# A fused decoder trunk's MLP weights rounded twice, once into SBUF and once into a PSUM bank for the subtraction

## The chip, the cores and the metric

The kernel runs on one core of one Trainium2 chip. The metric is the device time of one execution, in microseconds (us). Three runs of the kernel before gave 1218.43, 1218.79 and 1220.8 us; their median, 1218.79 us, is the time before.

## The reference

Two layers of a decoder trunk, all in fp32, on 512 tokens with a model width of 1024. Layer 0 mixes tokens by attention, layer 1 by a short gated convolution. Each mixer is followed by an MLP, and each sub-layer stands between two RMSNorms. The part that matters here is the MLP, 1024 to 4096 to 1024:

```python
def sq_relu_mlp(h, w_up, w_down):
    return jnp.square(jax.nn.relu(h @ w_up)) @ w_down
```

A norm scales each row by the inverse root of its mean square and by a gain vector; the MLP's input h is such a normed residual. A gated per-layer embedding closes each layer.

## The kernel before, in words

**Products.** TensorE multiplies in a rounded 32-bit type (fp32r) and the result has to be close to fp32, so every operand is held as a pair: `hi`, the value rounded to fp32r, and `lo`, what the rounding left out. `mm3` (L266 to L272) issues three matmuls for each product: hi·hi (L268), lo·hi (L269) and hi·lo (L270). It also counts the columns that TensorE has been given, and runs work that was put off until a given count.

**Splitting.** `split` (L274) makes a pair: ScalarE casts the source to `hi` (L276), and another engine, VectorE unless told otherwise, subtracts `hi` from the source to get `lo` (L277). Each 128 x 512 fp32 weight tile is split in this way; the trace calls its parts `raw`, `wh` and `wl`. The same two lines split the normed activations (`hTh`, `hTl`) and the MLP's hidden activations (`A11h`, `A12h`, `S1h`, `S3h` and their low parts).

**Weights.** All weight tiles stand in one list in the order of use. `wide` and `narrow` ask for a tile, and `prepare` (L175) then begins every tile up to eight (`SOON`) behind it: it fetches the raw tile by SP's DMA queue, takes two SBUF pages for hi and lo, and splits it. Raw tiles share 14 buffers.

**PSUM.** There are eight banks, each of 128 x 512 fp32. `bank` (L83) takes one for every product, transpose or attention step, and the framework gives it back after its last reader.

**The MLP** (`mlp`, L957). The 4096 hidden columns are worked through in eight groups of 512. In each, `up` computes four column blocks f, each of 8 k-tiles times three matmuls on 512 tokens into one bank, then ScalarE's Relu `r` (L975) and Square `q` (L961). Group 0 does this in two halves of 256 tokens, so that the first half can start before the last two token blocks are normed. Groups 0 to 6 multiply by the down weights with a Strassen-Winograd scheme of seven products. It takes sums of the hidden activations (`s`, made on GpSimd, L989) and of the down tiles (`T1` to `T4`, in the trace `dn_T`, made on GpSimd, L168). `down` (L1003) runs the products in the order 1, 2, 4, 5, 6, 7, 3; each takes two banks, called `dn_10`, `dn_11`, `dn_20` and so on, and four products of three matmuls. In group 0, ScalarE copies the two banks into `acc` pages (L1018); in groups 1 to 6, VectorE adds them there (L1021). Group 7 is plain. Eight of a group's fourteen down operands are such T pages. In groups 1 to 6 GpSimd makes their low parts; in group 0 VectorE does.

**Around the MLP.** Before layer 0's MLP, attention's output blocks are normed and added to the residual, block after block of 128 tokens (`om` L366 and `xb` L373 on VectorE). Then `pre_norm` (L344) takes the squares on ScalarE (L312), the inverse root on GpSimd (L307), and the scaled rows `n_h` (L328) on VectorE. TensorE transposes them into a bank `n_p` (L337), and `keep` splits that bank into hTh and hTl. The transposes are put off by a number of TensorE columns, so that TensorE has other work meanwhile. The first T page waits for the last n_h.

**What sets the order.** The program is written once, in order; a scheduler in the framework then places every engine's instructions into one fixed queue per engine by its own estimates. Each engine runs its queue in order, so an instruction that waits holds up everything behind it.

Of the kernel before, what the change touches and what calls it, by code (L numbers as in the profile page):

```python
# [9 lines left out]
F32R = mybir.dt.float32r  # L10
AF = mybir.ActivationFunctionType
ALU = mybir.AluOpType
# [56 lines left out]
def trunk(ctx: ExitStack, tc, x, xT, pT, g, gT, wv, wqk, bf, wo, wci, wcq, cw, wco, wup, wdn, wpp, wpg, out):  # L69
    nc = tc.nc  # L70
# [12 lines left out]
    def bank(name):  # L83
        return psum.tile([P, S], F32, tag="ps", name=name)
# [90 lines left out]
    def prepare(upto, lows=None):  # L175
        while begun[0] < min(upto, len(order)):
            n = begun[0]
            begun[0] += 1
            key, at = order[n]
            for of in (key[:3], key[:2]):  # L180
                if of in recipes:
                    derive(of)
            hi, lo = page(f"wh{n}", F32R), page(f"wl{n}", F32R)
            if isinstance(at, tuple):
                raw, w = derived.pop(key), S
                eng = nc.gpsimd if (key[0] == "dn" and key[2] > 0) or key[-1] in ON_POOL else nc.vector
            else:
                fetch(at + 1)
                raw, eng, w = fetched[at], lows or nc.vector, loads[at].shape[-1]
                fetched[at] = None  # L190
            if key[0] in ("v", "qk"):
                split_gained(hi, lo, raw, w, key[2], eng, key[0] == "qk" or key[1] == 2)
            else:
                split(hi[:, :w], lo[:, :w], raw[:, :w], eng)
            ready[key] = Pair(hi[:, :w], lo[:, :w])
# [78 lines left out]
    def split(hi, lo, src, eng=nc.vector):  # L274

        nc.scalar.copy(hi, src)  # L276
        return eng.tensor_tensor(out=lo, in0=src, in1=hi.bitcast(F32), op=ALU.subtract)  # L277

    def split_gained(hi, lo, src, w, at, eng, paired):

        parts = [(slice(0, w), at)]
        if paired:
            parts = [(slice(256 * i, 256 * i + 256), 2 * at + i) for i in range(2)]
        for c, k in parts:
            nc.scalar.mul(hi[:, c], src[:, c], first_g[:, k : k + 1])
        for c, k in parts:
            eng.scalar_tensor_tensor(
                out=lo[:, c], in0=src[:, c], scalar=first_g[:, k : k + 1],
                in1=hi[:, c].bitcast(F32), op0=ALU.mult, op1=ALU.subtract,
            )  # L290
# [1029 lines left out]
```

## Time and profile before

| what | value |
|---|---|
| runs | 1218.43, 1218.79, 1220.8 us |
| span of the profiled execution | 1216.5 us |
| median of the runs less this span | 2.3 us |
| TensorE (PE) busy | 1205.5 us, 99% |
| weight loads (PEld) busy | 1027.5 us, 84% |
| VectorE (DVE) busy | 931.4 us, 77% |
| ScalarE (ACT) busy | 691.4 us, 57% |
| GpSimd (POOL) busy | 655.4 us, 54% |
| HBM traffic | 120 GB/s over the span |

The profile is one execution; its own time is the span, and what lies around it (start and end of the program) is the difference from the runs' times. A group's row reads: line, engine, operation, output<-inputs, partitions x elements and types, count | busy time, mean ns of one | idle time of the engine just before them, and what ended most of it. A row of a timeline reads: start in us, length in us, engine, line, operation, count, and in brackets the idle time before it and what released it. A row of the waits reads: engine, instruction, what it waited for: us in total, times, longest. A row of windows gives each engine's busy time in a stretch of the span. A row of one line's instructions gives count, then minimum, median and maximum duration in ns, and the first and last start. Matmuls overlap, so one takes less time from start to start than its own length.

### The profile page before, as it was taken

Reading aid. Unit: us, or ns where it says so; the run is one execution under the profiler, and the core shown is the slowest. Engines: PE = TensorE matmul, PEld = TensorE weight load, DVE = VectorE, ACT = ScalarE, POOL = GpSimd, SP = SyncE. Lnnn points to the kernel's source line nnn. Section 1 sums busy time; section 2 is a strip of 40 time slices with the busy share of each in tenths; the row PEclk is TensorE's granted clock in tenths of the full one; section 3 lists DMA queues with packets and bytes.
Section 4 is the critical chain, followed back from the end, with each engine's and each line's share of the span. In section 5 each row is a group of like instructions: output and inputs, shape, how many; then the busy total and the mean of one; then the engine's idle time right before and its main releaser. Section 6 shows DMA issues by size and latency. Waiting matters only on the chain.

```text
span 1216.5 us, 18743 instructions
## 1 busy us (share of the span) xinstructions
PE 1205.5 (99%) x6175; PEld 1027.5 (84%) x6175; DVE 931.4 (77%) x1474; ACT 691.4 (57%) x1465; POOL 655.4 (54%) x616
## 2 busy tenths in 40 slices
PE   9999999999999999999999999999999999999997
PEld 8888887898888888888889999989888888888886
DVE  7888889586669766879877888866876787669873
ACT  7687778458644564455665534545746445645551
POOL 2035666155787877774213455126676878678210
PEclk9999999999999999999999999999999999999999
DMA  9376544623234323438223123542422443135401
GB/s 333 122 210 172 167 152 125 222 93 94 77 113 138 102 66 110 139 97 276 83 88 108 35 80 103 176 154 71 139 87 65 127 138 106 61 112 185 162 13 58
DMA packets 87314, 150.84 MB, mean 124 GB/s; under 512 B 10352, under 2 KB 18080, under 8 KB 87216
## 3 DMA queue, kind: packets, MB, share of 16 engines
q1 hardware_dynamic: 86640, 149.11, 39.3%
q8 instruction: 49, 0.80, 0.3%
q10 hardware_dynamic: 576, 0.53, 0.1%
q14 instruction: 49, 0.40, 0.1%
HBM read 139.03 MB, written 6.37 MB: 120 GB/s over the span
## 4 chain that ended last, share of the span: by engine, by line
PE 91%; ACT 3%; issue 2%; DVE 2%; POOL 1%; DMA 0%; SPq 0%; POOLq 0%; DVEq 0%; ACTq 0%
PE up L269 9%; PE up L270 9%; PE up L268 9%; PE dn L268 8%; PE dn L270 8%; PE dn L269 8%; PE v L476 3%; PE pg L269 2%; PE pg L268 2%; PE pg L270 2%; PE qk L270 2%; PE qk L269 2%; PE qk L268 2%; PE pT L590 1%; PE co L269 1%
## 5 line engine op out<-in xcount | busy, mean ns | idle before, releaser
L277 DVE TENSOR_TENSOR wl<-raw,wh 128x512 fp32r<-128x512 f32 x346 | 344.7, 1041 | 14.1 <-ACT wh L276 13.4
L269 PE MATMUL up<-hTh,wl 128*128 128x512 f32 (+1 forms) x576 | 210.2, 365 | 0.0
L270 PE MATMUL up<-hTl,wh 128*128 128x512 f32 (+1 forms) x576 | 209.6, 365 | 0.0
L268 PE MATMUL up<-hTh,wh 128*128 128x512 f32 (+1 forms) x576 | 208.7, 366 | 0.0
L276 ACT CAST wh<-raw 128x512 fp32r<-128x512 f32 x346 | 189.4, 625 | 4.5 <-DVE xd L373 4.4
L975 ACT ACTIVATE r<-up 128x512 f32<-128x512 f32 (+1 forms) x72 | 39.5, 548 | 201.8 <-PE up L270 190.1
L277 POOL TENSOR_TENSOR wl<-dn_T,wh 128x512 fp32r<-128x512 f32 x96 | 132.7, 1416 | 30.0 <-ACT wh L276 30.0
L168 POOL TENSOR_TENSOR dn_T<-raw,raw 128x512 f32<-128x512 f32 x56 | 87.0, 1564 | 69.1 <-DMA raw<-in_wdn 50.5
L269 PEld LDWEIGHTS up<-hTh,wl 128*128 128x128 f32 x576 | 108.6, 189 | 17.5
L268 PEld LDWEIGHTS up<-hTh,wh 128*128 128x128 f32 x576 | 108.6, 189 | 17.5
L270 PEld LDWEIGHTS up<-hTl,wh 128*128 128x128 f32 x576 | 108.2, 189 | 17.4
L1021 DVE TENSOR_TENSOR acc<-dn,acc 128x512 f32<-128x512 f32 x168 | 107.4, 680 | 13.9 <-PE dn L270 13.9
L168 POOL TENSOR_TENSOR dn_T<-raw,dn_T 128x512 f32<-128x512 f32 x56 | 92.5, 1651 | 2.2
L276 ACT CAST wh<-dn_T 128x512 fp32r<-128x512 f32 x112 | 61.4, 616 | 10.9 <-POOL dn_T L168 10.9
L277 DVE TENSOR_TENSOR A12l<-q,A12h 128x512 fp32r<-128x512 f32 x28 | 23.2, 829 | 53.8 <-ACT A12h L276 53.8
L1035 POOL TENSOR_TENSOR acc<-acc,acc 128x512 f32<-128x512 f32 x28 | 46.9, 1707 | 9.9 <-DVE acc L1021 9.9
L277 DVE TENSOR_TENSOR A11l<-q,A11h 128x256 fp32r<-128x256 f32 x28 | 23.2, 828 | 36.5 <-ACT A11h L276 36.5
L270 PE MATMUL qk<-hTl,wh 128*128 128x512 f32 x128 | 50.7, 396 | 0.0
L269 PE MATMUL pg<-wh,hTl 128*128 128x512 f32 x128 | 50.5, 394 | 0.0
L268 PE MATMUL pg<-wh,hTh 128*128 128x512 f32 x128 | 50.4, 394 | 0.0
L268 PE MATMUL qk<-hTh,wh 128*128 128x512 f32 x128 | 50.3, 393 | 0.0
L269 PE MATMUL qk<-hTh,wl 128*128 128x512 f32 x128 | 50.2, 392 | 0.0
(404 smaller groups left out, 3304.5 us busy)
## 6 DMA issues: line engine op xcount, KB each, us to landing
raw<-in_wup SPq DMA_DIRECT2D x128, 256.0 KB, 2.9
raw<-in_wdn SPq DMA_DIRECT2D x128, 256.0 KB, 2.8
raw<-in_wcq SPq DMA_DIRECT2D x36, 256.0 KB, 2.8
raw<-in_wqk SPq DMA_DIRECT2D x32, 256.0 KB, 5.3
raw<-in_wpg SPq DMA_DIRECT2D x32, 256.0 KB, 4.1
g<-in_g SPq DMA_DIRECT2D x22, 256.0 KB, 5.9
prl<-neg_c SPq DMA_DIRECT2D x16, 256.0 KB, 6.3
raw<-in_wo SPq DMA_DIRECT2D x16, 256.0 KB, 4.7
```

What stands on the lines that cost most here:

```text
L168: ins = nc.gpsimd.tensor_tensor(out=B[name], in0=B[a], in1=B[b], op=op)
L268: nc.tensor.matmul(ps, a.hi, b.hi, start=start, stop=False)
L269: nc.tensor.matmul(ps, a.lo, b.hi, start=False, stop=False)
L270: nc.tensor.matmul(ps, a.hi, b.lo, start=False, stop=stop)
L276: nc.scalar.copy(hi, src)
L277: return eng.tensor_tensor(out=lo, in0=src, in1=hi.bitcast(F32), op=ALU.subtract)
L476: nc.tensor.matmul(ps[:, : V_CHUNKS[c][1]], getattr(of_x(k, t), p), getattr(ready["v", c, k], of), start=k == 0 and p == of, stop=k == KT ...
L590: nc.tensor.transpose(ps[:, b * P : (b + 1) * P], probs[h][b][:, j * P : (j + 1) * P], ident)
L975: nc.scalar.activation(r[:, :n], ps[:, :n], AF.Relu)
L1021: ins = nc.vector.tensor_tensor(out=a, in0=banks[s], in1=a, op=ALU.add)
L1035: nc.gpsimd.tensor_tensor(out=a, in0=a, in1=acc[i, s][:, :S], op=ALU.add)
```

## The change

For tiles of the MLP's up and down weights whose low part VectorE makes, `prepare` calls a new function. ScalarE still casts the raw tile to `hi`, but also a second time into a PSUM bank, and VectorE subtracts the bank in place of the SBUF page. There is one such bank per layer, `beside0` and `beside1`; it is taken at the layer's first such tile, late in the mixer, and kept until the layer's last one. There are 128 tiles of up and 116 of down, 244 in all.

```diff
             if key[0] in ("v", "qk"):
                 split_gained(hi, lo, raw, w, key[2], eng, key[0] == "qk" or key[1] == 2)
+            elif key[0] in ("up", "dn") and eng is nc.vector:
+                split_beside(hi[:, :w], lo[:, :w], raw[:, :w], f"beside{key[1]}")
             else:
                 split(hi[:, :w], lo[:, :w], raw[:, :w], eng)
...
+    besides = {}
+
+    def split_beside(hi, lo, src, name):
+
+        if name not in besides:
+            besides[name] = bank(name)
+        again = besides[name][:, : src.shape[-1]]
+        nc.scalar.copy(again.bitcast(F32R), src)
+        nc.scalar.copy(hi, src)
+        nc.vector.tensor_tensor(out=lo, in0=src, in1=again, op=ALU.subtract)
```

In the changed kernel the second cast is L288, the cast to `hi` L289 and the subtraction L290; lines above them move by 2, lines below by 13. The scheduler also orders the queues anew. The counts on TensorE, VectorE and GpSimd stay; ScalarE has 244 instructions more.

Three places. First VectorE's queue at the end of layer 0's mixer, where `n_h_0` and `n_h_1` are the two halves of the model width of one token block (the first pair here is that of block 1), `n_p_0` and `n_p_1` are the transposed halves, and the number behind om is the token block. Before:

```order
L328 SCALAR_TENSOR_TENSOR n_h_0_3549<-xb_0_3427,n_r_y,g_2_0_3443 128x512
L328 SCALAR_TENSOR_TENSOR n_h_1_3551<-xb_1_3428,n_r_y,g_2_1_3444 128x512
L366 TENSOR_TENSOR om_2_3580<-o_2_3553,g_1_1_3440 128x512
L366 TENSOR_TENSOR om_3_3609<-o_3_3582,g_1_1_3440 128x512
L277 TENSOR_TENSOR wl_3612<-raw_3613,wh_3611 128x512
L366 TENSOR_TENSOR om_2_3644<-o_2_3617,g_1_0_3439 128x512
L373 SCALAR_TENSOR_TENSOR xb_1_3432<-om_2_3580,or_r_y,xb_1_3432 128x512
L277 TENSOR_TENSOR hTl<-n_p_0_3680,hTh 128x4x128
L373 SCALAR_TENSOR_TENSOR xb_0_3431<-om_2_3644,or_r_y,xb_0_3431 128x512
L277 TENSOR_TENSOR hTl<-n_p_1_3687,hTh 128x4x128
L277 TENSOR_TENSOR hTl<-n_p_0_3697,hTh 128x4x128
L277 TENSOR_TENSOR hTl<-n_p_1_3704,hTh 128x4x128
```

The same place of the changed kernel:

```order
L279 TENSOR_TENSOR hTl<-n_p_0_3689,hTh 128x4x128
L341 SCALAR_TENSOR_TENSOR n_h_0_3557<-xb_0_3427,n_r_y,g_2_0_3443 128x512
L341 SCALAR_TENSOR_TENSOR n_h_1_3559<-xb_1_3428,n_r_y,g_2_1_3444 128x512
L279 TENSOR_TENSOR hTl<-n_p_1_3696,hTh 128x4x128
L379 TENSOR_TENSOR om_2_3588<-o_2_3561,g_1_1_3440 128x512
L379 TENSOR_TENSOR om_3_3617<-o_3_3590,g_1_1_3440 128x512
L290 TENSOR_TENSOR wl_3620<-raw_3621,beside_3451 128x512
L379 TENSOR_TENSOR om_2_3653<-o_2_3626,g_1_0_3439 128x512
L386 SCALAR_TENSOR_TENSOR xb_1_3432<-om_2_3588,or_r_y,xb_1_3432 128x512
L279 TENSOR_TENSOR hTl<-n_p_0_3706,hTh 128x4x128
L279 TENSOR_TENSOR hTl<-n_p_1_3713,hTh 128x4x128
L386 SCALAR_TENSOR_TENSOR xb_0_3431<-om_2_3653,or_r_y,xb_0_3431 128x512
```

The first hTl, that of block 0, moved ahead of block 1's n_h, and its second half ahead of om. Further on, the first hTl of block 2 moved ahead of block 3's n_h in the same way.

Second, TensorE's queue in group 0 of layer 0, the end of the products dn_50 and dn_51 and the start of dn_60. Before, each bank's second half:

```order
L268 MATMUL dn_0_50_4190<-wh_3891,S1h_0_3_4104 128x512
L268 MATMUL dn_0_51_4191<-wh_3891,S1h_0_3_4104 128x512
L269 MATMUL dn_0_50_4190<-wh_3891,S1l_0_3_4105 128x512
L270 MATMUL dn_0_50_4190<-wl_3892,S1h_0_3_4104 128x512
L269 MATMUL dn_0_51_4191<-wh_3891,S1l_0_3_4105 128x512
L270 MATMUL dn_0_51_4191<-wl_3892,S1h_0_3_4104 128x512
L268 MATMUL dn_0_60_4220<-wh_4114,S1h_0_1_4030 128x512
```

The same place of the changed kernel:

```order
L270 MATMUL dn_0_50_4213<-wh_3907,S1h_0_3_4121 128x512
L271 MATMUL dn_0_50_4213<-wh_3907,S1l_0_3_4122 128x512
L272 MATMUL dn_0_50_4213<-wl_3908,S1h_0_3_4121 128x512
L270 MATMUL dn_0_51_4214<-wh_3896,S1h_0_1_4047 128x512
L271 MATMUL dn_0_51_4214<-wh_3896,S1l_0_1_4048 128x512
L272 MATMUL dn_0_51_4214<-wl_3897,S1h_0_1_4047 128x512
L270 MATMUL dn_0_51_4214<-wh_3907,S1h_0_3_4121 128x512
L271 MATMUL dn_0_51_4214<-wh_3907,S1l_0_3_4122 128x512
L272 MATMUL dn_0_51_4214<-wl_3908,S1h_0_3_4121 128x512
L270 MATMUL dn_0_60_4245<-wh_4131,S1h_0_1_4047 128x512
```

All six matmuls of dn_51 now stand behind dn_50's last, straight ahead of dn_60; before, dn_51's first three stood 18 rows further up.

Third, ScalarE's queue at the copies of group 0's first products into acc. Before:

```order
L276 CAST S3h_0_3_4108<-s_0_2_4066 128x512
L276 CAST wh_4114<-dn_0_T_0_3773 128x512
L276 CAST wh_4124<-dn_0_T_1_3781 128x512
L1018 COPY acc_1_0_4134<-dn_0_10_4112 128x512
L1018 COPY acc_1_1_4136<-dn_0_11_4113 128x512
L276 CAST wh_4140<-dn_0_T_0_3771 128x512
L276 CAST wh_4150<-dn_0_T_1_3779 128x512
L1018 COPY acc_2_0_4160<-dn_0_20_4138 128x512
```

The same place of the changed kernel:

```order
L278 CAST S3h_0_3_4125<-s_0_2_4083 128x512
L289 CAST wh_4131<-dn_0_T_0_3782 128x512
L289 CAST wh_4142<-dn_0_T_1_3790 128x512
L288 CAST beside_3451<-dn_0_T_1_3790 128x512
L1031 COPY acc_1_0_4153<-dn_0_10_4129 128x512
L1031 COPY acc_1_1_4155<-dn_0_11_4130 128x512
L289 CAST wh_4159<-dn_0_T_0_3780 128x512
L288 CAST beside_3451<-dn_0_T_0_3780 128x512
L289 CAST wh_4170<-dn_0_T_1_3788 128x512
L288 CAST beside_3451<-dn_0_T_1_3788 128x512
L1031 COPY acc_2_0_4181<-dn_0_20_4157 128x512
```

A beside cast stands ahead of the first copy, and two between one pair of copies and the next. The beside cast of T_0_3782 stands much further up, ahead of A11h_0_2.

## The prediction

> **What bounds the kernel now.** I read the page first, then busy time by windows, then the waits, then the timelines of the MLP's first groups. The page's times of the engines, and its costliest group:
>
> ```profile
> span 1216.5 us, 18743 instructions
> PE 1205.5 (99%) x6175; PEld 1027.5 (84%) x6175; DVE 931.4 (77%) x1474; ACT 691.4 (57%) x1465; POOL 655.4 (54%) x616
> L277 DVE TENSOR_TENSOR wl<-raw,wh 128x512 fp32r<-128x512 f32 x346 | 344.7, 1041 | 14.1 <-ACT wh L276 13.4
> ```
>
> TensorE is busy for all but 11 us; VectorE and ScalarE have room on average, and averages hide stages. The windows show group 0 of layer 0's MLP, groups 1 to 6, and group 0 of layer 1:
>
> ```profile
> core 0: us, PE busy (x) PEld busy (x) DVE busy (x) ACT busy (x) POOL busy (x), PEclk, DMA share, GB/s
> 262.00:300.00 38.00, 37.87 (x218) 32.69 (x217) 28.09 (x31) 28.80 (x62) 21.31 (x19) 1.00 0.29 92
> 300.00:542.00 242.00, 242.00 (x1070) 200.44 (x1069) 178.17 (x213) 126.61 (x232) 187.20 (x145) 1.00 0.34 105
> 830.00:870.00 40.00, 40.00 (x231) 35.00 (x230) 30.08 (x33) 30.88 (x65) 24.11 (x20) 1.00 0.31 93
> ```
>
> From 300 us on TensorE never pauses: 242.00 us for 1070 matmuls, 0.226 us each, at full clock. What VectorE saves there cannot shorten anything. So a gain is bounded by the small waits of group 0, where ScalarE is at 28.8 of 38 us. Those waits, between 262 and 300 us, are:
>
> ```profile
> PEld dn L268 <- ACT A12h L276: 0.6, 1, 0.6
> PEld dn L268 <- ACT acc L1018: 0.4, 1, 0.4
> ```
>
> Both are waits for ScalarE, the engine that gets the new work; the second is for a PSUM bank. A gain is at most about 1 us a layer.
>
> **The unit costs.** The change adds 244 casts to ScalarE (128 of up, 84 raw and 32 other tiles of down), takes no instruction away, and makes them share one bank: cast n+1 waits until subtraction n has read it. A subtraction now takes one operand from PSUM:
>
> ```profile
> L277 DVE TENSOR_TENSOR wl<-raw,wh x346: 673/685/1844, 157.0 to 1175.0; 128x512 fp32r<-128x512 f32 x173
> L277 DVE TENSOR_TENSOR hTl<-n_p,hTh x32: 676/681/694, 248.3 to 1178.2; 128x512 fp32r<-128x512 f32 x32
> ```
>
> hTl reads a bank (n_p) and takes 0.68 us, never over 0.69. The median wl takes 0.685 too; only its stretched ones make the mean 1041 ns. So I take 0.68 us: the change removes the stretch, up to 0.36 x 244 = 88 us of VectorE time, none of which TensorE waits for after 300 us. [...]
>
> ScalarE writing a PSUM bank is not in the trace. Its casts to SBUF follow each other at 0.53 us and take 0.60 to 0.62 alone (its rows below); its copies out of a bank, under the same matmul traffic, keep the same 0.53, so I see no reason for a dearer one. Below, an ACTIVATE on half the elements (273.66, below) takes 0.37. A gain is excluded, since each cast is added. I take 0.60. One tile's chain is then cast 0.60 + handoff 0.05 + subtraction 0.68 + handoff 0.08 = 1.41 us (1.18 by the lower bound), where it was one cast of 0.53. The handoffs are those from A12h's end to the matmul at 282.71 and from a copy's end to the one at 287.03, both below.
>
> [...]
>
> **(a) The mixer's tail, layer 0.** Transposes on TensorE (n_p), casts, and VectorE's rows:
>
> ```profile
> 246.73 1.03 PE L337 MATMUL n_p<-ident,n_h 128*128 128x128 f32 x8
> 248.30 1.04 PE L337 MATMUL n_p<-ident,n_h 128*128 128x128 f32 x8
> 250.56 0.28 PE L268 MATMUL up<-hTh,wh 128*128 128x256 f32 x1
> 259.20 1.91 PE L337 MATMUL n_p<-ident,n_h 128*128 128x128 f32 x16
> 260.87 0.36 PE L268 MATMUL up<-hTh,wh 128*128 128x256 f32 x1
> 247.37 1.08 ACT L276 CAST hTh<-n_p 128x512 fp32r<-128x512 f32 x2 [1.85 <-PE n_p L337]
> 238.58 1.42 DVE L328 SCALAR_TENSOR_TENSOR n_h<-xb,n_r_y,g 128x512 f32<-128x512 f32 x2 [2.00 <-POOL n_r_y L307]
> 243.92 1.41 DVE L328 SCALAR_TENSOR_TENSOR n_h<-xb,n_r_y,g 128x512 f32<-128x512 f32 x2 [2.00 <-POOL n_r_y L307]
> 248.31 0.68 DVE L277 TENSOR_TENSOR hTl<-n_p,hTh 128x512 fp32r<-128x512 f32 x1
> 249.57 1.88 DVE L277 TENSOR_TENSOR hTl<-n_p,hTh 128x512 fp32r<-128x512 f32 x3
> 258.47 1.42 DVE L328 SCALAR_TENSOR_TENSOR n_h<-xb,n_r_y,g 128x512 f32<-128x512 f32 x2 [2.66 <-POOL n_r_y L307]
> ```
>
> Seven tiles are prepared here. At 0.88 us more each the chain puts token block 0 back by up to 6 us; its n_h (238.58) has 6.7 us until TensorE wants it (246.73), so this is covered. What isn't covered is VectorE's new order: hTl of block 0 stands ahead of n_h of block 1, and TensorE transposes block 1 straight after block 0. Before, n_h of block 1 was ready at 245.3. Now: transposes of block 0's first half end at 247.3, its cast at 247.9, hTl at 248.6, the two n_h at 249.3 and 250.0; the second transposes end about 1.4 us later. Then block 1's hTl comes behind om, om, wl, om and xb: I put hTl of its first half at 254.4 where it was near 250.9, 3.5 in all, about 1.7 to 2.1 beyond the 1.4; I take 1.7. The same happens to block 3, whose n_h now waits for hTl of block 2: cast 260.44, hTl 261.1, n_h 261.8 and 262.4, transposes to 263.1 instead of 260.87, 2.3 us. Sum 5.4 us. In layer 1 these rows hardly change order: 0.
>
> **(b) Group 0's ScalarE chain.** GpSimd makes eight dn_T pages once the last n_h is there, and ScalarE waits for them:
>
> ```profile
> 260.02 2.55 POOL L168 TENSOR_TENSOR dn_T<-raw,raw 128x512 f32<-128x512 f32 x2 [1.58 <-DVE n_h L328]
> 293.60 1.30 POOL L168 TENSOR_TENSOR dn_T<-raw,raw 128x512 f32<-128x512 f32 x1 [8.80 <-DMA raw<-in_wdn]
> 272.10 1.66 ACT L276 CAST wh<-dn_T 128x512 fp32r<-128x512 f32 x3 [5.71 <-POOL dn_T L168]
> 273.66 0.37 ACT L975 ACTIVATE r<-up 128x256 f32<-128x256 f32 x1
> 277.13 0.62 ACT L276 CAST A12h<-q 128x512 fp32r<-128x512 f32 x1
> 278.10 1.07 PE L268 MATMUL dn<-wh,A12h 128*128 128x512 f32 x4
> 282.71 1.20 PE L268 MATMUL dn<-wh,A12h 128*128 128x512 f32 x4
> ```
>
> Eight pages took 12.1 us (260.02 to 272.10); at the 1.30 of one that ran beside little else they take 10.4, so the change gives 1.7 back. Their start moves by 3.1 (the first two terms) + 2.6 = 5.7, their end by 4.0. Then, where three casts took 1.56 (272.10 to 273.66), a cast, two waits of a whole chain and a last beside (0.53 + 2 x 1.41 + 0.60) take 3.95, and a fourth beside stands ahead of A11h (0.53): 2.9 more. ScalarE is 6.9 late at both A12h. The second one's reader (282.71) already waited for it, so TensorE is 6.9 late there, 1.5 beyond (a). Layer 1: its last n_h 0.8 late behind the one late subtraction, -1.7, +2.9 = 2.0.
>
> **(c) The bank.** Group 0's products occupy eight banks until ScalarE copies the first two to acc:
>
> ```profile
> 284.83 0.62 ACT L276 CAST S3h<-s 128x512 fp32r<-128x512 f32 x1 [0.20 <-POOL s L989]
> 285.36 1.14 ACT L276 CAST wh<-dn_T 128x512 fp32r<-128x512 f32 x2
> 286.40 1.06 ACT L1018 COPY acc<-dn 128x512 f32<-128x512 f32 x2
> 288.40 1.08 ACT L1018 COPY acc<-dn 128x512 f32<-128x512 f32 x2
> 287.03 0.50 PE L268 MATMUL dn<-wh,S1h 128*128 128x512 f32 x1
> 854.36 1.06 ACT L1018 COPY acc<-dn 128x512 f32<-128x512 f32 x2
> 854.98 0.50 PE L268 MATMUL dn<-wh,S1h 128*128 128x512 f32 x1
> ```
>
> The ninth bank's first matmul (287.03) starts right after the first copy ends (286.95). With seven, it is the eighth, dn_51, that waits, and the order has its six matmuls behind that copy: by the old times it could start at 285.6 (287.03 less 6 x 0.226). The copy comes later too: a beside cast stands ahead of it that waits for a subtraction queued behind S3l, until 286.8, so the copy ends near 288.0. TensorE waits 2.4 us. Layer 1's rows (854.36, 854.98) are the same pair: 2.4 again.
>
> **(d) The rest of group 0's steps.** ScalarE's step was two casts and two copies, 2.0 us (286.40 to 288.40); TensorE's is 12 x 0.226 = 2.72. Now: copies 1.06, cast 0.53, a full chain 1.41, beside 0.5 = 3.5, and the copies free the banks for later steps. Three steps at 0.75: 2.25 a layer, and group 1 starts some 0.5 late.
>
> **Groups 1 to 6.** One group's ScalarE rows:
>
> ```profile
> 406.09 7.39 ACT L276 CAST wh<-raw 128x512 fp32r<-128x512 f32 x14
> 423.45 0.60 ACT L975 ACTIVATE r<-up 128x512 f32<-128x512 f32 x1 [9.96 <-PE up L270]
> 428.83 0.60 ACT L975 ACTIVATE r<-up 128x512 f32<-128x512 f32 x1 [3.67 <-PE up L270]
> 439.71 0.60 ACT L975 ACTIVATE r<-up 128x512 f32<-128x512 f32 x1 [2.48 <-PE up L270]
> ```
>
> Fourteen tiles stretch by 14 x 0.88 = 12.3 us; the idle 9.96 + 3.67 + 2.48 = 16.1 covers it: 0. Group 7's tiles are prepared under the same lookahead: 0. SP's and POOL's queues keep their order, so no load or dn_T page moves against its neighbours.
>
> **Sum.** Layer 0: 5.4 + 1.5 + 2.4 + 2.25 + 0.5 = 12.05. Layer 1: 2.0 + 2.4 + 2.25 + 0.5 = 7.15. Span 1216.5 + 19.2 = 1235.7; the runs' median, 1218.79, lies 2.3 over this span (what lies around it), so 1238.0 us.
>
> **Rivals.** One: only (a) and (b) count, 5.4 + 1.5 + 2.0 = 8.9 us, 1227.7. It needs beside casts near the lower bound, and copies that reach ScalarE ahead of them; for it speaks that a chain of 1.18 leaves a step of (d) only 0.5 over TensorE's; against it, that the order puts dn_51 behind the copy whatever a cast costs. 0.16. Two: ScalarE becomes the bound in every group. VectorE's 14 additions to acc (about 0.6 us each, as its other rows) share its queue with the subtractions; were none hidden behind a cast, they would add 8.4 us to the chain. Above 45% of that (16.1 - 12.3 = 3.8) the idle time is used up; at six tenths ScalarE is 1.2 us late a group, and 12 such groups make 14 us more: 1252. Against it: an addition fits into the 0.6 us of each cast. 0.12. Three, the other side: VectorE's relief decides. GpSimd gives back 1.7 us a layer, n_h and hTl find VectorE free, and the lookahead of eight tiles covers every new wait; then only the 0.4 to 1 us of group 0's waits is at stake: 1217 to 1219. It decides if TensorE's wait for block 1's transposes stays under 0.3 us, which the order speaks against. 0.07. Four: the change doesn't relieve VectorE, because the stretch isn't from the shared operand. Then a chain is 1.77 us, the 1.7 isn't given back (3.4), (b) to (d) grow by some 6 x 0.36 a layer (4.3), and fourteen tiles stretch by 17.4 against 16.1 of idle time (1.3 x 12 = 16): 1262. 0.05.
>
> **Numbers.** The forecast, 1231 to 1245 by the bounds of its terms (a cast of 0.37 takes some 5 us off, half a chain at each of the new waits of (a) some 5 on), has 0.60. The range, 1224 to 1252, takes in rival one and the nearer half of two: 0.82. A difference of 0.2%, 2.4 us, is about what runs of this kernel can tell from none. Rival three splits into faster 0.02 and same 0.05; slower has 0.93.
>
> **What would show it.** After: beside casts near 0.6 us and 1.4 apart, wl near 0.68, VectorE's busy time down by up to 88 us; TensorE waits of 1 to 3 us at n_p and up before the MLP, one of 2.4 at dn_51 for an acc copy, and none in groups 2 to 6. No waits for acc would make (c) and (d) wrong; pauses in every group would make rival two right; a span below 1220 would make the sum wrong altogether.

## The result and the profile after

Four runs of the changed kernel gave 1260.07 to 1263.25 us, median 1262.2; four of the kernel before gave a median of 1219.0. The ratio is 1.035 (95%: 1.0336 to 1.0365). The forecast was 1238.0 with a range of 1224 to 1252: the sign is right, the loss is 43 us where 19 were predicted. First the page of the changed kernel, then all subtractions of its line 290:

```profile
span 1261.2 us, 18827 instructions
PE 1221.9 (97%) x6175; PEld 1032.5 (82%) x6175; DVE 818.6 (65%) x1474; ACT 831.2 (66%) x1709; POOL 598.2 (47%) x616
L290 DVE TENSOR_TENSOR wl<-raw,beside 128x512 fp32r<-128x512 f32 x228 | 156.4, 686 | 119.5 <-ACT beside L288 117.0
L288 ACT CAST beside<-raw 128x512 fp32r<-128x512 f32 x228 | 134.7, 591 | 90.5 <-DVE wl L290 90.4
```

```profile
L290 DVE TENSOR_TENSOR wl<-raw,beside x228: 671/689/691, 225.0 to 1162.7; 128x512 fp32r<-128x512 f32 x114
```

The change does what it says. VectorE's busy time falls from 931.4 to 818.6 us, its stretched subtractions are gone (at most 691 ns, once up to 1844), and GpSimd is 57 us less busy. ScalarE gains 140 us of work, and the two engines wait for each other: 117 us of VectorE for the cast, 90 us of ScalarE for the subtraction. None of that says where the 45 us of span come from, since TensorE's own instructions are the same 6175. TensorE's waits do (the line that waited, what it waited for, us in total, times, longest), after and then before:

```profile
PEld n_p L350 <- DVE n_h L341: 10.5, 6, 4.4
PEld dn L270 <- ACT acc L1031: 8.5, 8, 2.0
PEld dn L270 <- ACT A12h L278: 4.1, 4, 1.6
PEld pg L271 <- DVE hTl L279: 3.3, 2, 2.3
PEld dn L270 <- ACT r L988: 2.7, 4, 1.1
PEld c L271 <- DVE wl L279: 2.0, 2, 1.3
```

```profile
PEld dn L268 <- ACT A12h L276: 0.9, 2, 0.6
PEld dn L268 <- ACT acc L1018: 0.7, 2, 0.4
```

The second and third are group 0's, as predicted. The first and fourth are the surprise: most of the n_p waits, and all at pg, lie where a layer closes, at the transposes of its last norm and the gate of the per-layer embedding. The fifth is group 0's as well: a bank that ScalarE's Relu gives back late (0.5 us before). The last lies in layer 1's mixer. The windows of the changed kernel show the same, and the row behind them is the kernel before at the end of its layer 0:

```profile
core 0: us, PE busy (x) PEld busy (x) DVE busy (x) ACT busy (x) POOL busy (x), PEclk, DMA share, GB/s
240.00:300.00 60.00, 51.92 (x326) 44.39 (x325) 32.15 (x50) 38.98 (x87) 24.70 (x30) 1.00 0.21 74
300.00:560.00 260.00, 259.03 (x1139) 213.46 (x1139) 147.67 (x226) 189.84 (x344) 173.38 (x152) 1.00 0.35 106
598.00:624.00 26.00, 20.30 (x85) 15.69 (x84) 17.58 (x28) 12.75 (x33) 7.71 (x14) 0.87 0.08 27
840.00:900.00 60.00, 55.43 (x337) 47.27 (x336) 30.67 (x46) 45.00 (x94) 25.16 (x28) 1.00 0.27 83
1188.00:1200.00 12.00, 8.06 (x28) 6.42 (x27) 8.44 (x14) 6.94 (x18) 3.79 (x8) 0.72 0.01 2
```

```profile
590.00:616.00 26.00, 26.00 (x127) 21.49 (x126) 20.89 (x34) 18.24 (x39) 2.96 (x6) 1.00 0.32 101
```

In groups 1 to 6 (300 to 560 us) TensorE is busy 259.03 of 260 us. At the layers' ends (598 and 1188 us) it stands idle and has less than its full clock, where before it never paused.

To put a number on each stage, I added up, over all matmuls, what the step from one start to the next is over the step usual for that width in the kernel before, where it is over by more than 0.03 us. Sums in us; "open" is all up to the mixer's tail, "tail" runs from the first transpose n_p to group 0's first down matmul, "mix 1" is layer 1's mixer, "L1 gr0" is its tail and group 0:

```
                          open  tail  gr0   gr1-6 end   mix1  L1    gr1-6 end
                                L0    L0    L0    L0          gr0   L1    L1   total
before                    14.6  0.3   0.8   0     0.6   0.8   0.6   0     0.6  18.3
after                     16.1  5.4   6.7   0.6  10.4   4.6   7.2   0.6   9.7  61.3
only_group0               15.0  5.4   6.0   0     0.6   0.8   6.6   0     0.6  35.0
only_group7               15.0  1.3   0.9   0     4.6   1.3   0.6   0     4.5  28.1
all_but_group7            15.2  5.4   6.5   0.5   0.8   4.4   7.2   0.5   0.7  41.2
groups_1_to_6             16.0  0.3   2.7   0     1.3   5.1   2.5   0     1.3  29.0
bank_held_only            16.7  1.2   1.9   0     0.6   0.8   1.8   0     0.6  23.6
before_hidden_major       15.1  0.3   0.9   0     7.8   1.3   0.9   0     8.9  35.1
change_token_major        14.6  5.4   6.6   0.6   2.8   4.5   7.2   0.5   2.7  44.9
only_group7_token_major   15.0  0.6   0.9   0     3.7   0.9   0.6   0     4.1  25.7
group0_old_vector_order   16.3  6.2   4.3   0     0.6   0.8   6.6   0     0.6  35.3
group0_both_old_orders    16.4  5.9   4.1   0     0.6   0.8   6.6   0     0.6  35.0
group0_down_only          14.6  1.7   5.1   0     0.6   0.9   5.3   0     0.6  28.8
two_banks                 14.8  2.4   6.9   0.3   1.7   5.1   5.2   0.7   4.5  41.7
second_cast_of_rounded    15.0  8.7   3.4   7.0   4.4   5.0   5.8   3.9   9.2  62.3
```

After minus before is 43.0: 17.6 in the tail and the two groups 0 (19.2 predicted there), 18.9 at the two ends, 3.8 in layer 1's mixer, 1.1 in groups 1 to 6, 1.5 in the opening, which varies by some 2 us between profiles whatever is changed.

**What happens at an end.** ScalarE's rows as it comes to group 7 of layer 0, before and after:

```profile
545.79 0.60 ACT L975 ACTIVATE r<-up 128x512 f32<-128x512 f32 x1 [10.38 <-PE up L270]
```

```profile
558.79 0.59 ACT L288 CAST beside<-raw 128x512 fp32r<-128x512 f32 x1 [0.20 <-DVE wl L290]
560.14 0.59 ACT L288 CAST beside<-raw 128x512 fp32r<-128x512 f32 x1 [0.20 <-DVE wl L290]
564.70 0.59 ACT L988 ACTIVATE r<-up 128x512 f32<-128x512 f32 x1
```

Before, ScalarE had waited 10.38 us for TensorE when the first hidden block's Relu could start. After, it comes to that Relu straight from its row of casts, 1.35 us apart, with no idle time in front: it is now behind TensorE. The group's hidden blocks come late, and TensorE's queue holds another order. Rows of it, before and after (in dn0_7_1_0 the 1 is the token block, in hh0_1 the 1 is the hidden block):

```
2757 L268 MATMUL dn0_7_0_0_7012<-wh231_6785,hh0_1_6892 128x512
2763 L268 MATMUL dn0_7_1_0_7112<-wh230_6773,hh0_0_6823 128x512
2786 L268 MATMUL dn0_7_0_0_7012<-wh233_6809,hh0_3_7006 128x512
2795 L270 MATMUL dn0_7_0_1_7013<-wl237_6906,hh0_3_7006 128x512
...
2756 L270 MATMUL dn0_7_1_0_7235<-wh230_6888,hh0_0_6942 128x512
2766 L270 MATMUL dn0_7_0_0_7135<-wh231_6901,hh0_1_7013 128x512
2820 L270 MATMUL dn0_7_0_0_7135<-wh233_6927,hh0_3_7129 128x512
2829 L272 MATMUL dn0_7_0_1_7136<-wl237_7028,hh0_3_7129 128x512
```

Both groups begin at row 2751. Before, token blocks 0 and 1 come first, with all their hidden blocks; after, the hidden blocks follow one another, each going through most of the token blocks before the next. Token block 0's last product stood 44 matmuls behind the first, and now stands 78 behind it: at 0.226 us each, 9.9 and 17.6 us. VectorE's rows show it, before and then after (the first sum into acc, then the scaled rows n_h of token blocks 0 and 3):

```profile
571.86 2.48 DVE L1078 TENSOR_TENSOR acc<-dn,acc 128x512 f32<-128x512 f32 x4 [1.85 <-PE dn L270]
...
579.39 1.42 DVE L328 SCALAR_TENSOR_TENSOR n_h<-xd,n_r_y,g 128x512 f32<-128x512 f32 x2 [0.27 <-POOL n_r_y L307]
...
599.73 1.42 DVE L328 SCALAR_TENSOR_TENSOR n_h<-xd,n_r_y,g 128x512 f32<-128x512 f32 x2 [1.99 <-POOL n_r_y L307]
```

```profile
592.86 0.69 DVE L1091 TENSOR_TENSOR acc<-dn,acc 128x512 f32<-128x512 f32 x1 [7.26 <-PE dn L272]
...
602.76 1.42 DVE L341 SCALAR_TENSOR_TENSOR n_h<-xd,n_r_y,g 128x512 f32<-128x512 f32 x2 [1.90 <-POOL n_r_y L320]
...
624.13 1.41 DVE L341 SCALAR_TENSOR_TENSOR n_h<-xd,n_r_y,g 128x512 f32<-128x512 f32 x2
```

Group 7's first down matmul was at 561.91 before and at 575.21 after, so block 0's n_h came 17.5 us behind it, and now 27.6. The four blocks' norms are one chain over three engines, 5.9 to 9 us a block, so the delay reaches block 3. Meanwhile TensorE's other work (pp, the embedding's products) runs out, and it waits at n_p and pg.

### The profile page after: what moved, and what is told of

Same layout as the page of the kernel before. It is cut to its first block, busy times and chain, and to the rows that moved or that the text cites. A ratio compares the mean times of both kernels' runs of the same rounds, so it can differ in the third digit from the quotient of the medians.

```text
span 1261.2 us, 18827 instructions
## 1 busy us (share of the span) xinstructions
PE 1221.9 (97%) x6175; PEld 1032.5 (82%) x6175; DVE 818.6 (65%) x1474; ACT 831.2 (66%) x1709; POOL 598.2 (47%) x616
## 5 line engine op out<-in xcount | busy, mean ns | idle before, releaser
L290 DVE TENSOR_TENSOR wl<-raw,beside 128x512 fp32r<-128x512 f32 x228 | 156.4, 686 | 119.5 <-ACT beside L288 117.0
L288 ACT CAST beside<-raw 128x512 fp32r<-128x512 f32 x228 | 134.7, 591 | 90.5 <-DVE wl L290 90.4
L289 ACT CAST wh<-raw 128x512 fp32r<-128x512 f32 x228 | 137.8, 618 | 0.0
L271 PEld LDWEIGHTS up<-hTh,wl 128*128 128x128 f32 x576 | 108.6, 189 | 17.5
L168 POOL TENSOR_TENSOR dn_T<-raw,raw 128x512 f32<-128x512 f32 x56 | 72.0, 1299 | 65.0 <-DMA raw<-in_wdn 41.8
L279 DVE TENSOR_TENSOR wl<-raw,wh 128x512 fp32r<-128x512 f32 x118 | 89.5, 795 | 9.1 <-ACT wh L278 7.2
L168 POOL TENSOR_TENSOR dn_T<-raw,dn_T 128x512 f32<-128x512 f32 x56 | 73.0, 1304 | 2.2
L278 ACT CAST wh<-raw 128x512 fp32r<-128x512 f32 x118 | 66.7, 622 | 3.6 <-PE dn L272 2.2
L1002 POOL TENSOR_TENSOR s<-q 128x256 f32<-128x256 f32 x28 | 25.1, 898 | 83.1 <-ACT q L974 83.1
L278 ACT CAST S1h<-s 128x512 fp32r<-128x512 f32 x28 | 17.4, 622 | 57.2 <-POOL s L1002 57.2
L278 ACT CAST wh<-dn_T 128x512 fp32r<-128x512 f32 x96 | 52.3, 616 | 0.0
L272 PE MATMUL pg<-wl,hTh 128*128 128x512 f32 x128 | 50.9, 399 | 0.0
```

What stands on the lines that cost most here:

```text
L168: ins = nc.gpsimd.tensor_tensor(out=B[name], in0=B[a], in1=B[b], op=op)
L271: nc.tensor.matmul(ps, a.lo, b.hi, start=False, stop=False)
L272: nc.tensor.matmul(ps, a.hi, b.lo, start=False, stop=stop)
L288: nc.scalar.copy(again.bitcast(F32R), src)
L290: nc.vector.tensor_tensor(out=lo, in0=src, in1=again, op=ALU.subtract)
L1002: sums = lambda out, a, b, op: nc.gpsimd.tensor_tensor(out=out, in0=a, in1=b, op=op)
```

## The experiments

The theory tested first: group 0 costs about what was predicted, and the rest comes from the turned order of group 7's down products. Rivals: the loss is ScalarE's load, or the single bank's handshake, spread over all groups.

**Which tiles carry the loss.** Three kernels apply the change to part of the groups (GR is the tile's group).

```diff
-elif key[0] in ("up", "dn") and eng is nc.vector:
+elif key[0] in ("up", "dn") and eng is nc.vector and GR == 0:   # == 7 and != 7 in the other two
```

> Second rounding into the bank only for the up and down tiles of group 0 of each layer (16 + 28 tiles less GpSimd's none: 44 in all); every other tile is split as before. Theory O: the 43 us are two separate losses, about 19 us in group 0 and the mixer's tail (the terms (a) to (d) of the prediction), and the rest because group 7's down products were put in another order on TensorE. Here group 7's order is that of before, so about 1219 + 19 = 1238 us (1234 to 1242), with the waits at n_p, A12h and acc in group 0 as in the full change, and none at the layer's end. Theory H: the cost is the handshake of the shared bank, spread over all 244 tiles at 43 / 244 = 0.18 us each: 44 tiles cost 8 us, 1227.

Measured 1235.37 us, ratio 1.0133 (1.0118 to 1.0148): +16.4, all of it in the tail and the two groups 0. The tail's waits on TensorE:

```profile
PEld n_p L350 <- issue: 1.9, 1, 1.9
PEld n_p L350 <- DVE n_h L341: 1.7, 3, 1.4
PEld up L272 <- DVE hTl L279: 1.6, 1, 1.6
```

Together 5.2 us.

> Second rounding into the bank only for group 7's up and down tiles of each layer (48 in all). Theory O: TensorE's order of group 7's down products becomes that of the full change, block 0 is finished late, and the norms and the gate that follow find nothing to hide behind: about 1219 + 20 = 1239 us (1234 to 1246), all of it lost near the two layers' ends, group 0 as before. Theory H: 48 tiles at 0.18 us: 1228.

Measured 1228.52 us, 1.0075 (1.0058 to 1.0091). The table puts it at the two ends, 3.9 us each, where the first theory has it, but at half the size: here ScalarE starts its chain only with group 7's tiles, and is less late: block 0's first sum comes 15.8 us behind group 7's first down matmul, in the full change 17.7. The number is the one that the expectation gives the rival, but it counts 48 tiles where the profile shows 32 casts to the bank; for 32 the rival's 0.18 us a tile gives 1225. The place is not the rival's either.

> The change for groups 0 to 6, group 7 split as before (196 of the 244 tiles). Theory O, now with the sizes measured: groups 1 to 6 cost nothing by themselves, so the time is that of group 0 alone, 1235 (1234 to 1238); what the full change loses beyond that (27 us) is all bound to group 7 being reached with the bank's chain still running. Theory H: every tile pays, so 196 of 244 tiles pay 35 of the 43 us: 1254.

Measured 1241.34 us, 1.0177 (1.0162 to 1.0192). The ends cost nothing (0.8 and 0.7), so the loss at the ends needs group 7's tiles. The 6 us over what was expected are mostly layer 1's mixer (3.6) and 1.0 in groups 1 to 6. Against the full change, group 7's tiles are worth 20.9 us; alone they cost 9.6. They cost more where ScalarE is late already when it comes to them, as far as these two runs tell. (The expectation counts 196 tiles; the profile shows 212, for which the rival gives 1256.)

> The change for groups 1 to 6 only (152 of the 244 tiles: 96 of up and 72 of down less none, by the planner's count). Theory O: these groups show no wait of TensorE in the full change, so the MLP itself costs nothing and gains nothing from VectorE's relief: 1219; what it may cost is the other order at layer 1's start that the run of all but group 7 showed (3.6 us at the products c), so 1219 to 1224. A gain from VectorE's shorter subtractions would give 1217 or less.

```diff
+elif key[0] in ("up", "dn") and eng is nc.vector and 0 < GR < 7:
```

Measured 1228.98 us, 1.0081 (1.0066 to 1.0096): a miss. Inside groups 1 to 6 the change does cost 0, but their first tiles are prepared during group 0's last steps and take the bank there (1.9 us in each layer), and layer 1's mixer loses 4.3, 1.4 of it in matmuls at half clock (see the last section). (The expectation counts 152 tiles; the profile shows 168.)

> Only the first and the last tile of each layer's MLP weights are rounded into the bank (4 in all), so the bank is held as long as in the full change, but there is no chain and no further cast. The bank term alone: dn_51 stands behind dn_50 as in the full change and waits for the first copy to acc, which comes as early as before: 1.3 us a layer, 1222 us (1220 to 1224), nothing at the layers' ends. If holding a bank were what the change costs, it would be above 1240.

```diff
+elif key[0] in ("up", "dn") and eng is nc.vector and (key[0], *key[2:]) in (("up", 0, 0), ("dn", 7, 1, 3)):
```

Only the first and the last tile of each layer use the bank, which is held between them. Measured 1222.74 us, 1.0025 (1.0015 to 1.0034). A PSUM bank taken for the MLP's length costs 3.3 us here, and no more.

**The layers' ends.** If the order of group 7's down products is the cause, it must cost the same without the change, and giving it back must return it.

> The kernel before, without any second rounding; only the loops of group 7's down products are turned, so that all eight banks get their products of one hidden block before the next one. Theory O: this order alone makes the layers' ends late, as block 0's sums are complete only near the end of the 96 matmuls: 8 us later in each layer, of which 6 to 11 us shows: 1231 to 1241. Theory H: the order of matmuls costs nothing by itself, since the same work is done on the same tiles: 1219, within 3.

```diff
+for f in range(4):
+    for t in range(NB):
+        for n in range(2):
...
+            mm3(eight[t, n], tokens_of(hs[f], t), w, f == 0, f == 3)
```

This is the kernel before, with group 7's down products written hidden block first. Measured 1233.56 us, 1.0118 (1.0097 to 1.0139), all of the loss at the ends (7.2 and 8.3 us more, of which 1.4 and 2.4 are matmuls at half clock behind the waits). Its waits and VectorE's rows:

```profile
PEld n_p L337 <- DVE n_h L328: 4.6, 4, 2.1
```

```profile
579.54 2.05 DVE L1081 TENSOR_TENSOR acc<-dn,acc 128x512 f32<-128x512 f32 x3 [8.51 <-PE dn L270]
...
587.81 1.42 DVE L328 SCALAR_TENSOR_TENSOR n_h<-xd,n_r_y,g 128x512 f32<-128x512 f32 x2 [0.70 <-POOL n_r_y L307]
```

Block 0's first sum is 7.7 us later than before (571.86), its n_h 8.4, and TensorE waits at the same place, with none of the change in the kernel.

> The full change, but group 7's down products are tied to the order of before: blocks 2 and 3 start only when blocks 0 and 1 are complete. Theory O: the ends of the layers get back most of their loss: 1262 less 14 to 20 = 1242 to 1248, with group 0's waits left. Theory H: the order was only a sign of late tiles; the same wait appears at group 7's hidden blocks or low parts instead: 1258 to 1266.

```diff
+if f == 0 and t > 1:    # first matmul of blocks 2 and 3 after the last ones of the blocks ahead
+    for other in [(t - 1, 0), (t - 1, 1)] + ([(0, 0), (0, 1)] if t == 2 else []):
+        tc.add_manual_dep(first.ins, ends[other].ins.name, ...)    # NoSync
```

The full change, with an ordering edge (no semaphore) that puts group 7 back into token blocks. Measured 1245.99 us, 1.0218 (1.0203 to 1.0233): 16.2 us come back, 14.6 of them at the ends by the table, where 4.3 of the 18.9 stay. What is left among its waits:

```profile
PEld dn L270 <- ACT acc L1032: 8.5, 8, 2.0
PEld pg L271 <- DVE hTl L280: 4.4, 2, 2.2
PEld n_p L351 <- DVE n_h L342: 1.7, 3, 1.4
```

The n_p wait falls from 10.5 to the tail's own 1.7; group 0's waits are untouched.

> As group 7 alone (1228.5 us), with its down products tied to the order of before. Theory O (TensorE's order): nearly all of the 9.6 us go, 1219 to 1222. Theory L (the hidden blocks and low parts come late because ScalarE is behind): TensorE waits inside group 7 instead, 1225 to 1229.

The same edge on the kernel with group 7's tiles alone. Measured 1226.83 us, 1.0061 (1.0046 to 1.0076): 7.5 us remain although the order is the old one. The first theory misses here, and theory L has the number but not the place: TensorE doesn't wait inside group 7 but at pg, for hTl. At the ends the order gives back 1.3 of 7.9 us, where it gave back 14.6 of 18.9 in the full change. VectorE's rows:

```profile
572.40 1.29 DVE L1103 TENSOR_TENSOR acc<-dn,acc 128x512 f32<-128x512 f32 x2 [5.13 <-PE dn L272]
...
581.54 0.68 DVE L280 TENSOR_TENSOR wl<-raw,wh 128x512 fp32r<-128x512 f32 x1
582.14 0.68 DVE L1103 TENSOR_TENSOR acc<-dn,acc 128x512 f32<-128x512 f32 x1
583.52 1.42 DVE L342 SCALAR_TENSOR_TENSOR n_h<-xd,n_r_y,g 128x512 f32<-128x512 f32 x2 [0.70 <-POOL n_r_y L321]
```

The sums start on time (9.7 us behind group 7's first down matmul), but n_h comes 11.1 us after them, where before it took 7.5: subtractions of the embedding's tiles, late behind ScalarE, now stand one by one between the steps of block 0's norm. So lateness of ScalarE reaches the end by two ways, TensorE's order and VectorE's; the second is read from these rows, and no run takes it away. Over the kernels of this table the loss roughly follows one quantity, when block 0's n_h comes (us from group 7's first down matmul; where the layers differ, both are given; the loss is TensorE's, in the 62 us after):

```
                          first sum   n_h block 0   n_h block 3   loss
before                    9.95        17.5          37.8          0.6
change_token_major        9.7         20.1          41.3          2.8
only_group7_token_major   9.7         20.8          41.7          3.7, 4.1
two_banks                 11.3, 12.7  19.8, 20.8    40.9, 43.1    1.7, 4.5
only_group7               15.8        24.6          43.8          4.5
second_cast_of_rounded    15.2, 17.2  24.5, 27.1    43.6, 48.4    4.4, 9.2
before_hidden_major       17.2        25.5          44.4, 45.6    7.8, 8.9
after                     17.7, 18.1  27.6, 27.8    48.9, 47.3    10.4, 9.7
```

**Group 0's tail.** The prediction put its 5.4 us on VectorE's new order: hTl of block 0 ahead of n_h of block 1.

> As the run with group 0 alone (1235.4 us), but in layer 0's mixer hTl of blocks 0 and 2 is tied behind n_h of blocks 1 and 3, as it stood before. Theory O: the waits of TensorE at n_p before the MLP (1.4 and 1.9 us in that run) go; block 1's hTl still stands behind om, om, wl and om, so about 1 to 1.5 us of the 5.4 stay: 1231 to 1232 us (1230 to 1233). If the mixer's tail was late because of the chain of casts and not because of the order, it stays at 1235.

```diff
+tc.add_manual_dep(low.ins, normed_to[name, t + 1].ins.name, NoSync)   # hTl of blocks 0, 2 after n_h of 1, 3
```

On the kernel with group 0 alone: 1235.31 us, 1.0135 (1.0118 to 1.0152): 15.8 over the kernel before, where it was 16.4. The wait moved on to blocks 2 and 3.

> As group 0 alone (1235.4 us), but in layer 0's mixer the queues of VectorE and ScalarE are both tied to the sequence of before: on ScalarE the squares of block 2 ahead of hTh of block 0, on VectorE om and xb of block 2 ahead of hTl of block 0, and hTl of blocks 0 and 2 behind n_h of blocks 1 and 3. The beside casts stay. Theory O (the two queues' order makes the tail late): the 5.4 us before the MLP go, 1230 (1229 to 1231.5). Theory D (the beside chain delays the blocks themselves, and any order only moves the wait): 1234 to 1236, with the wait at other blocks.

```diff
+ahead = [normed_to.get((name, t + 1))] + (last_gained if t == 0 else [])    # hTl of block 0 also after om of block 2
...
+tc.add_manual_dep(high.ins, last_squared[0].ins.name, ...)    # hTh of block 0 after the squares of block 2
```

With the old order on VectorE and ScalarE: 1235.17 us, 1.0125 (1.0109 to 1.0142), 15.9 over. In both runs a stop of TensorE in the tail was followed by 3.4 us at a granted clock of 0.50, whose matmuls lost 1.4 and 1.5 us; in the changed kernel the clock stayed at 1.00 there. Without that the tail would cost 4.8 and 4.4, by estimate from the table, against 5.4 with the new order, and group 0 fell from 6.0 to 4.3 and 4.1. So the order may be worth some 1 us of the tail, but it is not its main cause. VectorE's rows of the kernel before, and of this one, whose whole program is 1.5 us late there already:

```profile
233.37 1.89 DVE L366 TENSOR_TENSOR om<-o,g 128x512 f32<-128x512 f32 x3 [1.21 <-DMA g<-in_g]
```

```profile
230.66 0.69 DVE L291 TENSOR_TENSOR wl<-raw,beside 128x512 fp32r<-128x512 f32 x1 [4.65 <-ACT beside L289]
...
237.50 0.69 DVE L291 TENSOR_TENSOR wl<-raw,beside 128x512 fp32r<-128x512 f32 x1 [0.71 <-ACT beside L289]
238.10 1.88 DVE L410 TENSOR_TENSOR om<-o,g 128x512 f32<-128x512 f32 x3
...
243.30 1.42 DVE L344 SCALAR_TENSOR_TENSOR n_h<-xb,n_r_y,g 128x512 f32<-128x512 f32 x2 [1.99 <-POOL n_r_y L321]
...
264.80 1.42 DVE L344 SCALAR_TENSOR_TENSOR n_h<-xb,n_r_y,g 128x512 f32<-128x512 f32 x2 [2.65 <-POOL n_r_y L321]
```

The chains of the tiles prepared here run up to om of block 0 without a gap, 1.35 to 1.41 us apiece, and put it at 238.10 instead of 233.37: 3.2 us late beyond the 1.5. The blocks' norms are a chain here too, so block 3's n_h (258.47 before) is at 264.80, 4.8 late beyond the 1.5. TensorE transposed block 3 0.7 us after its n_h; there was no more slack.

> Second rounding only for group 0's down tiles (28 tiles in all: 14 a layer); the eight up tiles that are split in the mixer's tail are split as before, so that no beside cast stands in ScalarE's queue there. Theory D (the seven casts, each waiting for a subtraction, put the serial chain of the normed blocks back by some 3 us): the 5.4 us before layer 0's MLP go whole, although nothing else there is tied: 1229 to 1231. Theory O (it was only the sequence): no difference in forecast here, as the sequence is that of before too; with the run in which the sequence was restored and the casts stayed (1235.2), the pair decides. If it stays at 1235, neither is right.

```diff
+elif key[0] == "dn" and key[2] == 0 and eng is nc.vector:
```

Without group 0's up tiles, of which those seven are part: 1229.32 us, 1.0082 (1.0065 to 1.0099).

```profile
234.74 1.89 DVE L379 TENSOR_TENSOR om<-o,g 128x512 f32<-128x512 f32 x3 [2.61 <-DMA g<-in_g]
...
259.67 1.41 DVE L341 SCALAR_TENSOR_TENSOR n_h<-xb,n_r_y,g 128x512 f32<-128x512 f32 x2 [2.65 <-POOL n_r_y L320]
```

The block chain is back (om waits for its load again), and the tail's loss falls from 5.4 to 1.7. The order is the old one here too, so this run takes away casts and order together; the run before it took away the order alone, and the pair puts most of the tail on the casts.

**Load or handshake.** Three kernels keep the extra cast and change how it is tied to VectorE.

> The 244 second casts go to an SBUF page that nothing reads, and VectorE subtracts the first cast as before: ScalarE has the change's extra work, but there is no bank and no handshake. Theory L (ScalarE's load is what counts): casts at 0.53 us each put some 4 to 5 us a layer on group 0's chain and steps, and up to 5 at the ends: 1226 to 1236. Theory C (the chain through one bank counts, the casts don't): 1219 to 1223.

```diff
+again = junk[:, : src.shape[-1]]
+nc.scalar.copy(again, src)           # nobody reads it
 nc.scalar.copy(hi, src)
+nc.vector.tensor_tensor(out=lo, in0=src, in1=hi.bitcast(F32), op=ALU.subtract)
```

Measured 1296.94 us, 1.0635 (1.0619 to 1.0651): a miss of both, and not a clean test. The unread cast waits for nothing but the load, was queued right behind it, and ScalarE stood there:

```profile
ACT junk L286 <- DMA raw<-in_wdn: 69.4, 49, 5.6
```

> The 244 second casts read wh, not the raw tile, and go to a page that nothing reads; VectorE subtracts wh as before. So ScalarE has the change's extra work right behind each first cast, never ahead of a load, with no bank and no handshake. Theory L (ScalarE's extra work in its queue, with the orders that it brings, is most of the cost): the mixer's tail 5, group 0 some 4 a layer (two casts a tile take 1.06 us, not 1.41), the layers' ends 8 to 16: 1240 to 1250. Theory C (the chain through the one bank): 1219 to 1225.

```diff
+nc.scalar.copy(hi, src)
+nc.scalar.copy(junk[:, : src.shape[-1]], hi.bitcast(F32))   # nobody reads it
```

Here the unread cast stands behind the real one. Measured 1262.77 us, 1.0358 (1.0343 to 1.0374): as slow as the change, with no bank and no handshake, and above the range of theory L. But the table shows another sum: groups 1 to 6 lose 7.0 and 3.9 us, where the change loses 0.6. From its page and its waits:

```profile
L287 DVE TENSOR_TENSOR wl<-raw,wh 128x512 fp32r<-128x512 f32 x228 | 260.5, 1189 | 21.5 <-ACT wh L285 19.0
```

```profile
PEld dn L271 <- DVE A12l L279: 6.6, 7, 1.4
```

VectorE still subtracts from SBUF, at 1189 ns, and hands the low parts to TensorE too late. So ScalarE's load, without bank or handshake, is enough to cost at the ends and in the tail. By the difference of these two kernels VectorE's relief is worth about 10 us in groups 1 to 6, but only against that load; the two differ in the handshake as well, so this is an argument and not a measurement. The equal totals are a coincidence.

> The change with two banks a layer taken in turn, so that a cast waits for the subtraction before the last one; six banks are left. Theory C: without the wait ScalarE passes two casts a tile in 1.06 us in place of 1.34 to 1.41, group 7's hidden blocks come in time and TensorE's order there is nearly that of before: the ends cost 0 to 3 us in all; group 0 pays for two banks with some 7 us a layer (dn_50 now waits), the mixer's tail 2: 1238 (1233 to 1243). If the number of free banks ruled, it would be slower than the full change: above 1264.

```diff
-f"beside{key[1]}"
+f"beside{key[1]}_{n % 2}"
```

Measured 1242.99 us, 1.0184 (1.0169 to 1.0199), at the upper edge. Its page:

```profile
L290 DVE TENSOR_TENSOR wl<-raw,beside 128x512 fp32r<-128x512 f32 x228 | 146.7, 680 | 46.0 <-ACT beside L288 38.3
L288 ACT CAST beside<-raw 128x512 fp32r<-128x512 f32 x228 | 130.5, 595 | 63.9 <-DVE wl L290 62.4
```

VectorE's idle time before its subtractions falls from 119.5 to 46.0 us, ScalarE is less late, and the ends cost 1.7 and 4.5 instead of 10.4 and 9.7. The tail's 5.4 fall to 2.4. Layer 0's group 0 gains nothing (6.9), with a second bank taken from its products.

**The clock.** One run put waits on TensorE into the kernel before.

> The kernel before, in which VectorE copies one operand of group 3 (S1h) onto itself 9 times in layer 0 and 6 times in layer 1, so that TensorE has to stand idle in the middle of a full stretch. If an idle stretch itself lowers the clock that TensorE is granted, the stretch behind a stop of over about 2 us runs at 0.5 for some microseconds, there as at the layers' ends in the full change, and a stop of about 1 us is not followed by one. If the low clock belongs to the work at the layers' ends, it stays at 1.00 here. Time 1219 plus the stops, plus 1.5 to 2.5 us for each slow stretch.

```diff
+for _ in range((9, 6)[l]):
+    nc.vector.tensor_copy(out=held, in_=held)   # held = A["S1", 1].hi, in group 3
```

One run, 1222.44 us. TensorE hardly stood idle in groups 1 to 6 (0.5 us in all by the step count), so this decides nothing.

None of these versions beats the kernel before, whose TensorE is busy for all but 11 us.

## Why the prediction was wrong, point by point

- **Unit costs: right.** A cast to the bank takes 0.591 us on average (0.60 taken), a chain 1.35 to 1.41 (1.41 taken), a subtraction 0.689 (0.68 taken), and the stretch is gone. A subtraction that reads the bank takes about as long as one that reads the SBUF page, 0.689 against 0.685 us in the median. Rival four, a stretch that stays, fell: none took over 0.691 us.
- **(a): size right (5.1 for 5.4), mechanism wrong in the main.** The step that failed is "so this is covered": the 6.7 us were block 0's own slack, but the blocks' norms are a chain, and its end had 0.7. Giving back the order returned 0.6 us of the time at most (some 1 us of the tail, if the half clock that followed is set aside); taking away the up tiles' casts returned 3.7 of the tail. TensorE's waits stood where the order put them (n_p and up), so the size agrees by luck: without the new order most of it is lost all the same.
- **(b): right.** Waits for A12h rose from 0.9 to 4.1 us in all, 3.2 more; 1.5 + 2.0 were predicted. At layer 0's second A12h TensorE starts at 291.20 where it was 282.71; less the 1.5 us that the opening lost, it is 7.0 us late for 6.9 predicted. The new waits themselves stand earlier, at the first A12h (1.60 and 1.33 us) and at the bank of the late Relu (r, 2.7 us in all for 0.5).
- **(c) and (d): right.** Waits for the acc copies are 8.5 us in all (0.7 before); 2 x (2.4 + 2.25) = 9.3 were predicted. The longest, 1.97 and 1.99 us, stand at dn_51, as predicted, and the three steps behind it wait 0.74 to 0.77 us for the 0.75 taken. With the bank held and no further casts these waits are 2.1 us in all.
- **Groups 1 to 6: right** for what was asked, 0.6 us a layer for 0. Rival two, ScalarE as the bound of every group, did not occur.
- **"Group 7's tiles are prepared under the same lookahead: 0": wrong, 18.9 us.** This is the step that broke the sum. In groups 1 to 6 the price of a late ScalarE is nothing, since TensorE has more columns to run. At the end of the MLP the same lateness decides the order of TensorE's and VectorE's queues and then the start of a chain of four norms, behind which TensorE has little left. That TensorE's order is the larger part of it in the full change (14.6 of 18.9 us) was shown from both sides (before_hidden_major, change_token_major); the rest, and most of what group 7's tiles cost alone, goes by VectorE's order as far as the rows of only_group7_token_major tell. That the framework turned it because the hidden blocks were estimated to come later is argued from ScalarE's rows, not shown.
- **Layer 1's mixer: no term, 3.8 us.** It appears wherever groups 1 to 6 carry the change, and in second_cast_of_rounded, and not with group 0 or 7 alone. Part of it is the 2.0 us wait of c for wl, and 0.8 us the half clock behind it. Why groups 1 to 6 bring it stays open.
- **Rivals one and three** needed less than the sum, and fell. None of the rivals names what happened; the range ended at rival two's price and not at a mechanism of the ends.

## What to carry to other kernels

Work hidden under a busy engine is only hidden while more of that engine's work follows; look at where each stretch ends, and ask what the lateness does to the order of the queues and to serial chains there. Slack is to be read at the last link of a chain, not at its first. Waits between two engines (here 90 and 117 us) say nothing of the price until one sees which of them TensorE stands behind.

## What the runs showed of the hardware

TensorE's stops at the layers' ends were followed by half its clock. The windows of the changed kernel at the end of layer 1:

```profile
1190.00:1192.00 2.00, 0.00 (x0) 0.00 (x0) 0.00 (x0) 1.91 (x7) 0.78 (x2) 1.00 0.01 4
1192.00:1194.00 2.00, 1.07 (x5) 1.07 (x6) 1.87 (x3) 0.55 (x2) 1.33 (x3) 0.55 0.00 0
...
1196.00:1198.00 2.00, 2.00 (x6) 1.61 (x5) 1.28 (x3) 1.43 (x5) 0.33 (x2) 0.50 0.00 0
```

After the stop the granted clock is 0.50 to 0.55 for some 6 us, with TensorE busy. Matmuls at about twice their usual step (at the ends 0.43 us from start to start, where 0.226 is usual) cost some 6 us of the 43 (2.8 and 2.4 at the ends, 0.8 in layer 1's mixer). The last of these shows that the stop need not be long. There TensorE waited 1.3 us at the longest, and the clock fell all the same:

```profile
680.00:682.00 2.00, 1.57 (x9) 1.28 (x8) 2.00 (x4) 2.00 (x6) 2.00 (x2) 0.55 0.40 131
```

In the 3.41 us ahead of the slow stretch, which is as long as it lasted, TensorE was busy for 1.86 us (676.77 to 680.18). Group 0's stops of up to 2.0 us had no such effect in the changed kernel (clock 1.00 in its windows), though TensorE was busy for only 1.68 us of a stretch of the same length there (263.76 to 267.17); in the two runs with the old orders a stop in the tail did (3.4 us at 0.50). So neither the longest stop nor the busy share tells the two cases apart here.

Between its opening and its end the changed kernel has four slow stretches, all at a granted clock of 0.50: from 605.1 and 618.7 us at the end of layer 0 and from 680.2 in layer 1's mixer, 3.4 us each, and from 1192.2 at the end of layer 1, 6.8 us. In the 3.41 us ahead of each TensorE was busy for 1.51, 1.44, 1.86 and 0.22 us, so only the last stands behind an almost idle stretch. What lowers the clock, and what gives it back, no run here shows.
